# HGRN2 scores in blocks of 32 or 64 tokens, written by column groups of TensorE

## The chip, the cores and the metric

One Trainium2 chip, of which the kernel uses one core. The metric is device time in microseconds (us); three runs of the kernel before have a median of 2869.47 us (2864.01 to 2870.82).

## The reference, cut to what matters

The program is one layer of a diffusion backbone over 256 context and 2048 latent tokens, with four parallel mixers. The change touches the HGRN2 mixer alone, a gated linear recurrence over four heads of 64 channels, in both directions of time:

```
def step(S, inp):
    qc, kc, vc, lf = inp
    b = jnp.cumsum(lf, axis=1)
    ...
    diff = jnp.minimum(b[:, :, None] - b[:, None, :], 0.0)
    decay = jnp.where(lower, jnp.exp(diff), 0.0)
    scores = jnp.einsum('bthk,bshk,btshk->bhts', qc, kc, decay)
    intra = jnp.einsum('bhts,bshv->bthv', scores, vc)
    S = jnp.exp(b_end)[..., None] * S + jnp.einsum('bshk,bshv->bhkv', kc * jnp.exp(b_end[:, None] - b), vc)
    return S, inter + intra
```

A score of query token t and key token s is a sum over channels of q times k times the product of all forget gates between the two tokens.

## The kernel before, in words

The 2304 tokens are five blocks: 256 context tokens and four times 512 latent tokens. The first pass makes q, the forget gates f and the values by matrix products, each in three matmuls (`gemm_cm`, lines 192 to 194: high times high, high times low, low times high part; `gemm_tm`, lines 579 to 581). The HGRN2 stage then calls `hgrn_local` ten times, for five blocks and two pairs of heads. One call holds both heads of a pair side by side, in chunks of 128 tokens: eight chunks of 128 columns for a latent block, four for the context block. The 128 partitions are 64 channels of the forward and 64 of the backward direction.

Within a chunk the scores are built in levels, as in a binary tree. Line 755 makes the level of the diagonal. For level lv from 0 to 6 the tokens are grouped in cells of 2^lv. ScalarE copies the half of q whose query token lies in the other cell of a pair into a zeroed tile z (lines 780 and 781). TensorE multiplies kt by z for each chunk, a full 128 by 128 square in PSUM (line 787). VectorE (forward half) and GpSimd (backward half) multiply kt by the gates, once for each half of the columns (line 791), and VectorE does the same to q (lines 792 and 793). Of each square only the entries whose two tokens lie in sibling cells belong to this level. For levels 0 to 4 VectorE copies them into `at` under a mask (line 808); for levels 5 and 6 ScalarE copies the off-diagonal blocks (line 806). The squares of one level are a tile of 128 by 1024 in PSUM, of which there are two (`psc`).

After level 6, TensorE transposes kt (line 814), multiplies the scores with the values (line 820) and makes the chunk states (line 829).

```
for i in range(hh * m, hh * m + m):
    s_ = slice(i * 128, i * 128 + 128)
    PE.matmul(sc[:, s_], kt[:, s_], z[:, s_], start=True, stop=True)
...
    V.copy_predicated(a3, masks_[:, lv, :].unsqueeze(1).to_broadcast([128, m2, 128]), s3)
```

Two calls are written in step: five steps of one alternate with five of the call before, so that levels 0 to 3 of one stand beside levels 4 to 6 and the tail of the other. The matrix products of the next call's inputs (`prep`) are written behind them. The order in which each engine issues is then set when the program is built, by a scheduler with its own estimate of durations; each engine works through its list in that order. After this stage come the second pass, the S5 mixer, the output product and the MLP, which last to the end.

Of the kernel before, what the change touches and what calls it, by code (L numbers as in the profile page):

```python
# [10 lines left out]
F32 = mybir.dt.float32  # L11
F32R = mybir.dt.float32r
I32 = mybir.dt.int32
AF = mybir.ActivationFunctionType
# [60 lines left out]
def trunk_kernel(ctx, tc, I, O):  # L75
    nc = tc.nc
    V, A, G, PE, SP = nc.vector, nc.scalar, nc.gpsimd, nc.tensor, nc.sync
# [10 lines left out]
    def nm(s):  # L88
        uid[0] += 1
        return f"{s}_{uid[0]}"  # L90
# [13 lines left out]
    def psc():  # L104
        return psums["s"].tile([128, 1024], F32, tag="ps", name=nm("psc"))
# [5 lines left out]
    def const(name, shape, src, dt=F32, pool=None, q=None):  # L111
        t = (pool or cst).tile(shape, dt, tag=name, name=name)
        (q or SP).dma_start(t, src)
        return t
# [620 lines left out]
    def hgrn_local(b, pair, qn, f, vt, p1, qz, Sx, masks_):  # L735
        t0, n, c = BLOCKS[b]
        n2 = 2 * n
        m = n // CH
        m2 = 2 * m
# [5 lines left out]
        kt, q, at = w("kt"), w("q"), w("at")  # L745
# [3 lines left out]
                SP.dma_start(q[64 * d:64 * d + 64, hh * n:(hh + 1) * n], qn[hh * 64:hh * 64 + 64, :n])  # L749
        G.tensor_scalar(kt[:, :n2], f, -1.0, 1.0, ALU.mult, ALU.add)  # L750
        V.tensor_scalar(f, f, F_MIN, None, ALU.max)
        sc = psc()
        for i in range(m2):
            s_ = slice(i * 128, i * 128 + 128)
            PE.matmul(sc[:, s_], kt[:, s_], q[:, s_], start=True, stop=True)
        V.tensor_tensor(q[:, :n2], q[:, :n2], f, ALU.mult)
        A.activation(at[:, :n2], sc[:, :n2], AF.Copy)
        yield
        tcur = f
        tnx = p1.tile([128, 768], F32, tag="tnx", name=nm("tnx"), bufs=2)  # L760
        a3 = at[:, :n2].rearrange("p (m t) -> p m t", t=128)
        for lv in range(7):
            cs = 1 << lv
            mm = n2 // (2 * cs)

            def v4(t, lo_, hi_, half):
                return t[lo_:hi_, :n2].rearrange("p (m two c) -> p m two c", two=2, c=cs)[:, :, half, :]

            tv = tcur.rearrange("p (m two) -> p m two", two=2)

            def tb(lo_, hi_, half):
                return tv[lo_:hi_, :, half:half + 1].to_broadcast([64, mm, cs])

            if lv < len(qz):
                z = qz[lv]
            else:
                z = p1.tile([128, 1024], F32, tag="qzr", name=nm("qzr"), bufs=2)
                G.memset(v4(z, 0, 64, 0), 0.0)
                G.memset(v4(z, 64, 128, 1), 0.0)
            A.activation(v4(z, 0, 64, 1), v4(q, 0, 64, 1), AF.Copy)  # L780
            A.activation(v4(z, 64, 128, 0), v4(q, 64, 128, 0), AF.Copy)
            sc = psc()
            hm = mm // 2
            for hh in range(2):
                for i in range(hh * m, hh * m + m):
                    s_ = slice(i * 128, i * 128 + 128)
                    PE.matmul(sc[:, s_], kt[:, s_], z[:, s_], start=True, stop=True)  # L787
                hs_ = slice(hh * hm, hh * hm + hm)
                for eng, lo_, hi_, half in ((V, 0, 64, 0), (G, 64, 128, 1)):
                    kv = v4(kt, lo_, hi_, half)[:, hs_, :]  # L790
                    eng.tensor_tensor(kv, kv, tb(lo_, hi_, 1 - half)[:, hs_, :], ALU.mult)  # L791
            V.tensor_tensor(v4(q, 0, 64, 1), v4(q, 0, 64, 1), tb(0, 64, 0), ALU.mult)
            V.tensor_tensor(v4(q, 64, 128, 0), v4(q, 64, 128, 0), tb(64, 128, 1), ALU.mult)
            if lv == 6:
                V.tensor_tensor(tot[:, 2 * pair:2 * pair + 2, c0:c0 + m],
                                tv[:, :, 0].rearrange("p (h m) -> p h m", h=2),
                                tv[:, :, 1].rearrange("p (h m) -> p h m", h=2), ALU.mult)
            else:
                nxt = tnx[:, 512 * (lv % 2):512 * (lv % 2) + mm]
                V.tensor_tensor(nxt, tv[:, :, 0], tv[:, :, 1], ALU.mult)  # L800
                tcur = nxt
            s3 = sc[:, :n2].rearrange("p (m t) -> p m t", t=128)
            if lv >= 5:
                for o_ in range(0, 128, cs):
                    x_ = o_ ^ cs
                    A.activation(a3[o_:o_ + cs, :, x_:x_ + cs], s3[o_:o_ + cs, :, x_:x_ + cs], AF.Copy)
            else:
                V.copy_predicated(a3, masks_[:, lv, :].unsqueeze(1).to_broadcast([128, m2, 128]), s3)
            yield
        SP.dma_start(qD[b][:, 2 * pair:2 * pair + 2, :], q[:, :n2].rearrange("p (h t) -> p h t", h=2))  # L810

# [13 lines left out]
        for hh in range(2):  # L825
            h = 2 * pair + hh
            for i in range(m):
                o_ = 512 + (hh * m + i) * 64
# [471 lines left out]
    def pool(stack, name, bufs=1, side="left"):  # L1300
        return stack.enter_context(tc.tile_pool(name=name, bufs=bufs, side=side))
# [20 lines left out]
    with ExitStack() as e1:  # L1322
# [46 lines left out]

        ready = [prep(0), prep(1)]  # L1370
        p1 = pool(e1, "p1")
        masks_ = const("masks", [128, 5, 128], I["masks"], I32, p1, SP)
        qz = [p1.tile([128, 1024], F32, tag=f"qz{lv}", name=f"qz{lv}") for lv in range(3)]
        for z in qz:
            G.memset(z, 0.0)
# [105 lines left out]
    p3 = pool(e5, "p3")  # L1481
    with ExitStack() as e:
        s5_out(1, pool(e, "so1"))
    pad = pool(e5, "pad").tile([128, 16], F32, tag="pad", name="pad")
    G.memset(pad, 0.0)
    h3a = pool(e5, "h3a", 9)
    fs = mlp_up(0, 3, h2, p30, h30, none)
# [129 lines left out]
```

## Time and profile before

| what | us |
|---|---|
| median of three runs | 2869.47 |
| the profiled execution, its own time | 2862.84 |
| its span, first to last instruction | 2860.9 |
| TensorE (PE) busy in the span | 2708.4 |
| VectorE (DVE) busy | 1887.5 |
| ScalarE (ACT) busy | 1108.4 |
| GpSimd (POOL) busy | 920.4 |

The first product of `hgrn_local` starts at 178 us of the span and its last ends at 628 us. In the profile one float32 matmul is two records of MATMUL and two of LDWEIGHTS, so eight chunks are sixteen records. A busy time is the time from a record's start to its modelled end; records overlap, so the pace of TensorE is read from the starts.

### The profile page before, as it was taken

Reading aid. Unit: us, or ns where it says so; the run is one execution under the profiler, and the core shown is the slowest. Engines: PE = TensorE matmul, PEld = TensorE weight load, DVE = VectorE, ACT = ScalarE, POOL = GpSimd, SP = SyncE. Lnnn points to the kernel's source line nnn. Section 1 sums busy time; section 2 is a strip of 40 time slices with the busy share of each in tenths; the row PEclk is TensorE's granted clock in tenths of the full one; section 3 lists DMA queues with packets and bytes.
Section 4 is the critical chain, followed back from the end, with each engine's and each line's share of the span. In section 5 each row is a group of like instructions: output and inputs, shape, how many; then the busy total and the mean of one; then the engine's idle time right before and its main releaser. Section 6 shows DMA issues by size and latency. Waiting matters only on the chain.

```text
span 2860.9 us, 38042 instructions
## 1 busy us (share of the span) xinstructions
PE 2708.4 (95%) x14376; PEld 2257.5 (79%) x14376; DVE 1887.5 (66%) x2766; ACT 1108.4 (39%) x1710; POOL 920.4 (32%) x809
## 2 busy tenths in 40 slices
PE   6798999899999879999999999999999999999998
PEld 3576878887777679987788888788887888888888
DVE  9879678956899976669873475943474334543336
ACT  4645455532333445442422343333343223423323
POOL 4435334612533533343231232211332111411113
PEclk8899999999999979999999999999999999999999
DMA  7784555688886756533333343333343234233333
GB/s 264 282 294 151 188 193 178 229 286 310 299 295 225 241 173 203 174 118 111 111 103 96 125 143 108 111 99 104 114 149 106 99 94 127 90 124 96 96 96 126
DMA packets 186279, 467.17 MB, mean 163 GB/s; under 512 B 40176, under 2 KB 70000, under 8 KB 173040
## 3 DMA queue, kind: packets, MB, share of 16 engines
q1 hardware_dynamic: 183936, 463.56, 48.8%
q8 instruction: 114, 1.87, 0.3%
q10 hardware_dynamic: 2160, 1.18, 0.1%
q14 instruction: 69, 0.57, 0.1%
HBM read 383.47 MB, written 77.53 MB: 161 GB/s over the span
## 4 chain that ended last, share of the span: by engine, by line
PE 62%; DVE 10%; DMA 2%; issue 1%; ACT 0%; SPq 0%; POOL 0%; DVEq 0%; ACTq 0%
PE pg L194 20%; PE pg L193 20%; PE pg L192 20%; DVE x L1184 3%; DVE m L997 1%; DVE whl L162 1%; DMA awt<-in_ada_w_dram 1%; DVE gg L1005 1%; DVE pa L289 0%; PE pb L1051 0%; DVE hh L1014 0%; DVE hh L1013 0%; DVE lo L304 0%; DMA t<-mixD 0%; PE pd L986 0%
## 5 line engine op out<-in xcount | busy, mean ns | idle before, releaser
L192 PE MATMUL pg<-hi,whl 128*128 128x512 f32 (+1 forms) x3488 | 1286.5, 371 | 10.2 <-ACT st L586 4.9
L194 PE MATMUL pg<-hi,whl 128*128 128x512 f32 (+1 forms) x3488 | 1286.2, 370 | 8.4 <-DVE whl L162 8.4
L193 PE MATMUL pg<-lo,whl 128*128 128x512 f32 (+1 forms) x3488 | 1287.0, 370 | 2.3 <-DVE lo L1245 2.3
L160 POOL TENSOR_TENSOR whl<-wraw,whl 128x512 fp32r<-128x512 f32 (+1 forms) x296 | 435.7, 1493 | 1193.5 <-ACT whl L156 1159.9
L192 PEld LDWEIGHTS pg<-hi,whl 128*128 128x128 f32 x3488 | 662.3, 190 | 130.6 <-issue 5.8
L194 PEld LDWEIGHTS pg<-hi,whl 128*128 128x128 f32 x3488 | 662.9, 190 | 125.8 <-DVE whl L162 8.9
L193 PEld LDWEIGHTS pg<-lo,whl 128*128 128x128 f32 x3488 | 663.4, 190 | 120.0 <-issue 6.9
L156 ACT ACTIVATE whl<-wraw 128x1024 fp32r<-128x1024 f32 (+1 forms) x396 | 415.3, 1051 | 588.1 <-PE pg L194 457.0
L162 DVE TENSOR_TENSOR whl<-wraw,whl 128x1024 fp32r<-128x1024 f32 x248 | 310.7, 1254 | 63.1 <-ACT whl L156 61.8
L1257 DVE SCALAR_TENSOR_TENSOR x<-pg,adaT,x 128x512 f32<-128x512 f32 (+1 forms) x168 | 111.8, 669 | 282.9 <-PE pg L194 282.4
L1242 DVE TENSOR_TENSOR t<-t 128x512 f32<-128x512 f32 (+1 forms) x160 | 114.1, 714 | 261.0 <-ACT t L1241 260.3
L1241 ACT ACTIVATE t<-pg 128x512 f32<-128x512 f32 (+1 forms) x160 | 88.7, 554 | 382.3 <-PE pg L194 379.6
L1184 DVE SCALAR_TENSOR_TENSOR x<-x,cvw 128x512 f32<-128x512 f32 (+1 forms) x300 | 216.3, 764 | 0.6
L1245 DVE TENSOR_TENSOR lo<-t,hi 128x512 fp32r<-128x512 f32 (+1 forms) x160 | 142.5, 891 | 35.0 <-ACT hi L1244 34.8
L791 POOL TENSOR_TENSOR kt<-kt,tnx 64x256 f32<-64x256 f32 (+1 forms) x120 | 100.9, 848 | 163.6 <-issue 126.4
L252 POOL TENSOR_TENSOR sq<-sq,sq 128x512 f32<-128x512 f32 (+1 forms) x56 | 87.3, 1559 | 125.6 <-ACT sq L248 125.6
L1244 ACT ACTIVATE hi<-t 128x512 fp32r<-128x512 f32 (+1 forms) x160 | 92.8, 581 | 82.1 <-DVE t L1242 82.1
L1225 DVE SCALAR_TENSOR_TENSOR x<-pg,adaT,x 128x512 f32<-128x512 f32 (+1 forms) x40 | 27.8, 694 | 110.9 <-PE pg L194 110.8
L248 ACT ACTIVATE sq<-x 128x512 f32<-128x512 f32 (+1 forms) x120 | 66.0, 553 | 75.9 <-DVE sq L252 17.4
L787 PE MATMUL psc<-qzr,kt 128*128 128x128 f32 x576 | 74.6, 281 | 10.7 <-DVE kt L791 7.0
L787 PEld LDWEIGHTS psc<-qzr,kt 128*128 128x128 f32 x576 | 70.4, 196 | 14.4 <-POOL kt L791 7.8
L303 ACT ACTIVATE hi<-hm,adaT 128x512 fp32r<-128x512 f32 (+1 forms) x72 | 49.5, 697 | 68.5 <-DVE hm L301 64.5
(373 smaller groups left out, 2919.6 us busy)
## 6 DMA issues: line engine op xcount, KB each, us to landing
wraw<-in_mlp_w_dram SPq DMA_DIRECT2D x328, 512.0 KB, 3.5
whl<-w_p2c_hl SPq DMA_DIRECT2D x32, 1024.0 KB, 7.6
whl<-w_p1c_hl SPq DMA_DIRECT2D x22, 1024.0 KB, 7.7
wraw<-in_w_out_dram SPq DMA_DIRECT2D x40, 512.0 KB, 3.6
awt<-in_ada_w_dram SPq DMA_DIRECT2D x32, 512.0 KB, 5.9
whl<-w_p1t_hl SPq DMA_DIRECT2D x12, 1024.0 KB, 4.9
x<-in_xT_dram SPq DMA_DIRECT2D x16, 512.0 KB, 6.4
aw<-in_ada_w_dram SPq DMA_DIRECT2D x8, 1024.0 KB, 7.2
```

The lines of the kernel that those rows point to most:

```text
L156: A.activation(hi[:, :w], raw[:, :w], AF.Copy)
L160: G.tensor_tensor(lo[:, h_], raw[:, h_], f32(hi[:, h_]), ALU.subtract)
L162: V.tensor_tensor(lo[:, :w], raw[:, :w], f32(hi[:, :w]), ALU.subtract)
L192: PE.matmul(ps[:, :n], wh, xh[:, ts], start=k == 0, stop=False)
L193: PE.matmul(ps[:, :n], wh, xl[:, ts], start=False, stop=False)
L194: PE.matmul(ps[:, :n], wl, xh[:, ts], start=False, stop=k == 7)
L787: PE.matmul(sc[:, s_], kt[:, s_], z[:, s_], start=True, stop=True)
L791: eng.tensor_tensor(kv, kv, tb(lo_, hi_, 1 - half)[:, hs_, :], ALU.mult)
L1184: V.scalar_tensor_tensor(acc[i][:, :n], u2[:, i, k:k + n], cvw[:, i, k:k + 1], acc[i][:, :n], ALU.mult, ALU.add)
L1242: V.tensor_tensor(r, r, r, ALU.mult)
L1245: V.tensor_tensor(lo, r, f32(hi), ALU.subtract)
L1257: V.scalar_tensor_tensor(x8[:, o, ts], ps[:, :n], adaT[:, 40 + o, c:c + 1], x8[:, o, ts], ALU.mult, ALU.add)
```

## The change

The helper `score` replaces the full square of a chunk by 128 / c products of c columns each, where c is 32 for the diagonal and levels 0 to 5, and 64 for level 6. The product of block j takes c tokens of kt as weights (128 partitions by c columns) and c tokens of q or z as moving operand. It writes partitions c*j to c*j + c of PSUM, so the blocks of one chunk lie in different column groups of the array, beneath each other, in c columns of the tile for each chunk. Levels 5 and 6 pair block j with its sibling (j ^ 1). The mask copy then covers 32 columns for each chunk and writes a new tile `al` (128 by 256), and four ScalarE copies behind level 4 bring `al` to the diagonal blocks of `at`. The masks are loaded as four pieces of 32 columns by four DMAs. A padding tile that stands ahead of the MLP's operand tiles grows from 64 to 448 bytes for each partition.

```diff
+        def score(sc, i, z, c, x):
+            for j in range(128 // c):
+                s_, t_ = (slice(i * 128 + c * r, i * 128 + c * r + c) for r in (j, j ^ x))
+                PE.matmul(sc[c * j:c * j + c, c * i:c * i + c], kt[:, s_], z[:, t_], start=True, stop=True)
+        def blocks(sc, c):
+            return sc[:, :c * m2].rearrange("p (m t) -> p m t", t=c)
         sc = psc()
         for i in range(m2):
-            s_ = slice(i * 128, i * 128 + 128)
-            PE.matmul(sc[:, s_], kt[:, s_], q[:, s_], start=True, stop=True)
+            score(sc, i, q, 32, 0)
-        A.activation(at[:, :n2], sc[:, :n2], AF.Copy)
+        A.activation(al[:, :32 * m2], sc[:, :32 * m2], AF.Copy)
...
-                    PE.matmul(sc[:, s_], kt[:, s_], z[:, s_], start=True, stop=True)
+                    score(sc, i, z, max(32, cs), lv >= 5)
...
-                    A.activation(a3[o_:o_ + cs, :, x_:x_ + cs], s3[o_:o_ + cs, :, x_:x_ + cs], AF.Copy)
+                    A.activation(a3[o_:o_ + cs, :, x_:x_ + cs], blocks(sc, cs)[o_:o_ + cs], AF.Copy)
             else:
-                V.copy_predicated(a3, masks_[:, lv, :].unsqueeze(1).to_broadcast([128, m2, 128]), s3)
+                V.copy_predicated(blocks(al, 32), masks_[:, lv, :].unsqueeze(1).to_broadcast([128, m2, 32]),
+                                  blocks(sc, 32))
+            if lv == 4:
+                for o_ in range(0, 128, 32):
+                    A.activation(a3[o_:o_ + 32, :, o_:o_ + 32], blocks(al, 32)[o_:o_ + 32], AF.Copy)
...
-        masks_ = const("masks", [128, 5, 128], I["masks"], I32, p1, SP)
+        masks_ = p1.tile([128, 5, 32], I32, tag="masks", name="masks")
+        for o_ in range(0, 128, 32):
+            SP.dma_start(masks_[o_:o_ + 32], I["masks"][o_:o_ + 32, :, o_:o_ + 32])
...
-    pad = pool(e5, "pad").tile([128, 16], F32, tag="pad", name="pad")
+    pad = pool(e5, "pad").tile([128, 112], F32, tag="pad", name="pad")
```

Because the scheduler's estimates change with the products, the issue order changes too, from the first call of `hgrn_local` to the middle of the context block's MLP. Two places show how. The first is TensorE's list where the second and third call stand side by side and no matrix product of `prep` is between the levels (`psc` is the scores' tile, `qz` and `qzr` are the z tiles, `kt_1902` belongs to the older call). Before:

```order
L755 MATMUL psc_2307<-q_2299,kt_2298 128x128 x8
L787 MATMUL psc_2323<-qzr_2318,kt_1902 128x128 x8
L256 MATMUL pa_2293<-sq_2270,ones 128x512
L787 MATMUL psc_2343<-qz_1538,kt_2298 128x128 x8
L787 MATMUL psc_2365<-qzr_2360,kt_1902 128x128 x8
L787 MATMUL psc_2387<-qz_1539,kt_2298 128x128 x8
L787 MATMUL psc_2409<-qzr_2404,kt_1902 128x128 x8
L787 MATMUL psc_2429<-qz_1540,kt_2298 128x128 x8
L814 MATMUL psc_2447<-ident,kt_1902 128x128 x8
L820 MATMUL psc_2457<-at_1904,vt_837 64x128 x8
L787 MATMUL psc_2483<-qzr_2478,kt_2298 128x128 x8
```

In the changed kernel (its line 758 is the helper's product, 814, 820 and 832 of it are `at<-psc`, `at<-al` and the old line 820):

```order
L758 MATMUL psc_2613<-q_2604,kt_2603 32x32 x32
L758 MATMUL psc_2653<-qzr_2648,kt_2026 32x32 x32
L758 MATMUL psc_2701<-qz_1541,kt_2603 32x32 x32
L758 MATMUL psc_2747<-qzr_2742,kt_2026 32x32 x32
L758 MATMUL psc_2793<-qz_1542,kt_2603 32x32 x32
L758 MATMUL psc_2839<-qzr_2834,kt_2026 64x64 x16
L758 MATMUL psc_2867<-qz_1543,kt_2603 32x32 x26
L256 MATMUL pa_2598<-sq_2575,ones 128x512
L758 MATMUL psc_2867<-qz_1543,kt_2603 32x32 x6
L826 MATMUL psc_2909<-ident,kt_2026 128x128 x8
L832 MATMUL psc_2919<-at_2028,vt_837 64x128 x8
L758 MATMUL psc_2945<-qzr_2940,kt_2603 32x32 x32
```

The levels keep their order and each row of eight squares becomes 32 small products, or 16 at level 6; only the sum of squares (L256) moved, to the inside of a level.

The second place is ScalarE's list at the same point of the program. Before:

```order
L780 ACTIVATE qzr_2404<-q_1903 64x8x64
L781 ACTIVATE qzr_2404<-q_1903 64x8x64
L780 ACTIVATE qz_1538<-q_2299 64x512
L781 ACTIVATE qz_1538<-q_2299 64x512
L287 ACT_TABLE_LOAD
L287 ACTIVATE pa_2293<-pa_2293,epsb 128x512
L780 ACTIVATE qz_1539<-q_2299 64x256x2
L781 ACTIVATE qz_1539<-q_2299 64x256x2
L806 ACTIVATE at_1904<-psc_2365 32x8x32 x4
```

In the changed kernel:

```order
L767 ACTIVATE al_2612<-psc_2613 128x256
L790 ACTIVATE qzr_2834<-q_2027 64x8x64
L791 ACTIVATE qzr_2834<-q_2027 64x8x64
L248 ACTIVATE sq_2586<-x_360_2562 128x512
L790 ACTIVATE qz_1541<-q_2604 64x512
L791 ACTIVATE qz_1541<-q_2604 64x512
L820 ACTIVATE at_2028<-al_2035 32x8x32 x4
L248 ACTIVATE sq_2589<-x_360_2562 128x512
L790 ACTIVATE qz_1542<-q_2604 64x256x2
L791 ACTIVATE qz_1542<-q_2604 64x256x2
L248 ACTIVATE sq_2592<-x_360_2562 128x512
L814 ACTIVATE at_2028<-psc_2747 32x8x32 x4
```

The four new copies of the older call (L820) stand ahead of the z copies of the younger call's level 1 (L790, L791), which were next to those of level 0 before.

## Rows read from the trace of the kernel before

**Rows 1.** The page's first part: busy time, share of the span, records.

```profile
PE 2708.4 (95%) x14376; PEld 2257.5 (79%) x14376; DVE 1887.5 (66%) x2766; ACT 1108.4 (39%) x1710; POOL 920.4 (32%) x809
```

**Rows 2.** Windows: stretch, length; busy PE, PEld, DVE, ACT, POOL; granted clock, DMA.

```profile
178.00:300.00 122.00, 101.00 (x618) 87.08 (x616) 111.85 (x157) 63.52 (x99) 53.08 (x62) 0.94 0.49 176
300.00:360.00 60.00, 58.98 (x347) 51.35 (x348) 38.30 (x64) 29.75 (x51) 20.98 (x24) 1.00 0.67 230
360.00:420.00 60.00, 53.60 (x342) 47.02 (x341) 51.84 (x93) 33.30 (x58) 24.05 (x28) 1.00 0.52 182
420.00:480.00 60.00, 59.47 (x376) 52.66 (x375) 40.54 (x70) 28.04 (x48) 21.25 (x30) 1.00 0.55 186
480.00:628.00 148.00, 131.70 (x1009) 121.08 (x1007) 123.48 (x265) 71.44 (x137) 69.54 (x99) 0.98 0.69 242
```

**Rows 3.** Waits from 178 to 630 us: total us, times, longest.

```profile
POOL kt L791 <- PE psc L787: 77.9, 35, 15.8
...
PE psc L787 <- DVE at L808: 8.0, 7, 3.8
```

**Rows 4.** Groups by line and shape: busy us, mean ns of one, idle before.

```profile
L787 PE MATMUL psc<-qzr,kt 128*128 128x128 f32 x576 | 74.6, 281 | 10.7 <-DVE kt L791 7.0 <-ACT kt L815 2.4 <-DVE at L808 0.9
L787 PE MATMUL psc<-qz,kt 128*128 128x128 f32 x432 | 57.5, 287 | 13.9 <-DVE at L808 7.1 <-DVE kt L791 2.8 <-ACT qz L781 2.1
...
L755 PE MATMUL psc<-q,kt 128*128 128x128 f32 x144 | 18.1, 277 | 3.0 <-POOL kt L750 2.7 <-issue 0.3
```

**Rows 5.** Timeline of TensorE: eight full squares between matrix products (start, us, what).

```profile
196.11 0.39 PE L193 MATMUL pg<-lo,whl 128*128 128x512 f32 x1
196.33 0.39 PE L194 MATMUL pg<-hi,whl 128*128 128x512 f32 x1
196.56 1.95 PE L787 MATMUL psc<-qz,kt 128*128 128x128 f32 x16
198.26 0.48 PE L192 MATMUL pg<-hi,whl 128*128 128x512 f32 x1
```

**Rows 6.** The same view: products in two column groups, between matrix products.

```profile
247.13 0.39 PE L581 MATMUL pg<-whl,hi 128*128 128x512 f32 x1
247.45 1.09 PE L820 MATMUL psc<-at,vt 128*64 128x128 f32 x16
248.48 0.50 PE L580 MATMUL pg<-whl,lo 128*128 128x512 f32 x1
```

**Rows 7.** The same view: products in four column groups of 32, in the S5 mixer.

```profile
693.79 0.40 PE L937 MATMUL pd<-tb,u 128*32 128x128 f32 x8
694.01 0.40 PE L937 MATMUL pd<-tb,dr 128*32 128x128 f32 x8
```

**Rows 8.** Timeline of weight loads: 128 columns each, for products of 32 moving columns.

```profile
659.02 3.76 PEld L893 LDWEIGHTS pd<-u,ta 128*128 128x128 f32 x32
```

**Rows 9.** Groups by shape of the copies out of the scores' tile.

```profile
L808 DVE COPY_PREDICATED at<-masks,psc 128x1024 f32<-128x1024 int32 x40 | 53.3, 1332 | 0.0
L808 DVE COPY_PREDICATED at<-masks,psc 128x512 f32<-128x512 int32 x10 | 7.2, 720 | 0.0
```

**Rows 10.** The same view on ScalarE.

```profile
L806 ACT ACTIVATE at<-psc 32x256 f32<-32x256 f32 x32 | 12.0, 375 | 5.5 <-PE psc L787 5.2
...
L757 ACT ACTIVATE at<-psc 128x1024 f32<-128x1024 f32 x8 | 8.2, 1024 | 6.6 <-PE psc L755 5.1 <-ACT vt L584 1.5
```

**Rows 11.** Windows of line 808 alone: VectorE's busy time in two of the stretches.

```profile
300.00:360.00 60.00, 6.92 (x6) 1.00 0.67 230
...
420.00:480.00 60.00, 8.07 (x6) 1.00 0.55 186
```

**Rows 12.** Windows of line 787 alone in the same two: TensorE, weight loads.

```profile
300.00:360.00 60.00, 13.57 (x112) 13.28 (x112) 1.00 0.67 230
...
420.00:480.00 60.00, 17.76 (x149) 17.50 (x150) 1.00 0.55 186
```

**Rows 13.** The window of the longest run of levels without matrix products.

```profile
272.00:296.00 24.00, 14.74 (x105) 13.88 (x105) 22.63 (x33) 10.37 (x17) 10.58 (x14) 0.86 0.15 44
```

More of the change, by code (lines that the diff above doesn't have):

```diff
@@ L751, in hgrn_local @@
         V.tensor_scalar(f, f, F_MIN, None, ALU.max)
+        al = p1.tile([128, 256], F32, tag="al", name=nm("al"), bufs=2)
+        def score(sc, i, z, c, x):
[4 more added lines that the diff above has]
+            return sc[:, :c * m2].rearrange("p (m t) -> p m t", t=c)
         sc = psc()
         for i in range(m2):
-            s_ = slice(i * 128, i * 128 + 128)
-            PE.matmul(sc[:, s_], kt[:, s_], q[:, s_], start=True, stop=True)
+            score(sc, i, q, 32, 0)
         V.tensor_tensor(q[:, :n2], q[:, :n2], f, ALU.mult)
-        A.activation(at[:, :n2], sc[:, :n2], AF.Copy)
+        A.activation(al[:, :32 * m2], sc[:, :32 * m2], AF.Copy)
         yield
@@ L785, in hgrn_local @@
                 for i in range(hh * m, hh * m + m):
-                    s_ = slice(i * 128, i * 128 + 128)
-                    PE.matmul(sc[:, s_], kt[:, s_], z[:, s_], start=True, stop=True)
+                    score(sc, i, z, max(32, cs), lv >= 5)
                 hs_ = slice(hh * hm, hh * hm + hm)
@@ L801, in hgrn_local @@
                 tcur = nxt
-            s3 = sc[:, :n2].rearrange("p (m t) -> p m t", t=128)
             if lv >= 5:
```

## The prediction

> **What bounds the kernel now.** I read the page's busy times first. TensorE is busy 95% of the span, VectorE 66% [rows 1]; for the whole program TensorE sets the end, so time is won only where its list gets shorter or stops waiting. The change works in the HGRN2 stage, 178 to 628 us, so I then read that stage in windows [rows 2]. The reader is to see two kinds of stretch. From 300 to 360 and 420 to 480 us TensorE is busy 59 of 60 us and VectorE 38 and 41: TensorE leads. In the other 330 us TensorE is busy 286 us and VectorE 287 us: there TensorE waits about 44 us, and VectorE is the busiest engine or its equal (112 of 122 us in the first). Over the stage TensorE is busy 405 of 450 us. The table of waits shows for what the engines wait: GpSimd's kt products wait 77.9 us in total for the scores, and TensorE waits 8.0 us for the mask copies to free a scores' tile [rows 3]. So scores, kt products and mask copies form a loop, and the change shortens two of its three parts.
>
> **Part 1: TensorE.** The scores are 576 + 432 + 144 = 1152 records [rows 4], 72 levels of sixteen (a context level counts as half of one). What a level costs now is read from starts: the matmul ahead of it starts at 196.33, the one behind it at 198.26, 1.93 us, of which 0.23 us is the pace of a 512-column matmul (196.11 to 196.33). So a level costs 1.70 us, 106 ns for each pass of 128 columns [rows 5].
>
> The new products have no row: no product here has 32 weight columns and 32 moving columns. I bound them by the nearest rows. Products in column groups of 32 stand in the S5 mixer: eight records, two passes in four groups, take 0.22 us from start to start [rows 7], 0.11 us for a pass of four groups, the same as one full pass. So the four groups work at once. Those products stream 128 columns, the new ones a quarter. Upper bound: 0.11 us for each pass of four groups, as if fewer columns saved nothing. Lower bound: a quarter, 0.027 us. Between them: weight loads of 128 columns, with products of only 32 columns behind each, follow each other every 3.76 / 32 = 0.118 us [rows 8], 0.011 more than the 0.107 of the load itself. The product is hidden beside the next load and a pass costs its longer side and 0.011. I take that row, as it has the same 32 moving columns: 0.027 + 0.011 = 0.038 us.
>
> The Trainium skill, "TensorE: Matmul & The Clock Gate", Part 1, has a rule against this: starts of matmuls never come closer than about 25 ns, however few columns there are. By it a level's 64 small products would take an estimated 1.6 us and the change would save TensorE nothing. Nothing above rests on that rule; it belongs to the last rival.
>
> To this comes a price for entering and leaving column groups. The products with the values run in two groups: 1.35 us from the matmul ahead to the one behind [rows 6], less 0.23 for that matmul and less 8 passes of 0.107, leaves 0.26 us. I charge it to every level, though some levels stand side by side without it.
>
> A new level of 32-column blocks: 16 passes of 0.038 and 0.26 are 0.87 us, 0.83 saved. Level 6, in blocks of 64 columns: 16 passes of 0.053 + 0.011 and 0.26 are 1.28 us, 0.42 saved. Seven levels of the first and one of the second save 0.78 us on average, 56 us for 72. With the upper bound a level costs 2.02 us, 0.32 more than now, 23 us more for 72.
>
> **Part 2: VectorE.** The mask copy takes 1332 ns for 1024 columns and 720 for 512 [rows 9], 1.195 ns for a column. For 256 columns that line gives 720 - 306 = 414 ns, 31% of now. All 50 copies fall from 60.5 us to some 19.
>
> **Part 3: ScalarE.** It gets four copies for each call from `al` to `at`, of 32 by 256, 375 ns each in the same form [rows 10]: 1.5 us, ten calls 14 us with two of half size. The diagonal's copy shrinks from 1024 ns to about a third. ScalarE is busy 226 of 450 us [rows 2], which hides the total. But the four wait for the last mask copy, and behind them on ScalarE stand the z copies of the younger call (second place of the order): at worst 1.5 us for each call, 15 us. TensorE needs them late, for the product with the values. I take 0 and keep 15 for the range.
>
> **Small parts.** Four mask loads in place of one lie between the same transfers in front of the stage's first level: 0. The wider padding only moves addresses of the MLP's operands: 0, no row prices it. Behind the stage the issue order is different up to the context block's MLP while the work is the same: 0, with 10 us either way.
>
> **The sum, stretch by stretch.** Where TensorE leads, its own saving counts: 112 + 149 records of line 787 [rows 12] are 16.3 levels, with their diagonal levels 18.6; times 0.78 are 14.5 us. Elsewhere I let only VectorE's saving count, since it is the smaller of the two: 60.5 us of mask copies less the 6.92 + 8.07 in those two stretches [rows 11] are 45.5 us, of which 69% go, 31.4 us. TensorE loses there 53.4 levels times 0.78, 41.7 us, so it does not stand in the way. Together 46 us. The profiled execution took 2862.84 us, with 1.9 us around its span, and would take 2817. The median of the runs shown, 2869.47, lies 6.6 us above it; I forecast that median: 2869.5 - 46 = **2823 us**. What is late next in the stage is the elementwise chain, VectorE's q products and GpSimd's kt products.
>
> **The rivals.**
> - *Both savings count everywhere.* TensorE's 56 us fall out, and of its 45 us of waiting about half goes, since the loop around the mask copies is shorter. 78 us, 2791. For it: TensorE's waits in the stage are for that loop. Against it: VectorE would be busier than any engine is now. Chance 0.15.
> - *The chain of kt products holds the other stretches.* A level cannot start before GpSimd has multiplied kt, and those 330 us keep their length. Only the 14.5 us count: 2855. For it: GpSimd's kt products stand first in the waits [rows 3]. Against it: they wait there for the scores themselves, which come earlier. Chance 0.12.
> - *The clock.* In the longest run of levels without matrix products, 272 to 296 us, the granted clock was 0.86 [rows 13], against 0.98 as the mean of the stage's windows [rows 2]. Smaller scores leave the array less to do. If the whole stage fell to 0.86, the 349 us that TensorE keeps would grow by 14%, 48 us, the whole gain: 2871, no change. Against it: the stretches full of matrix products show 1.00. Chance 0.08.
> - *Slower: the pace of issue.* The row of four groups also reads as one weight load and product every 27 ns [rows 7]. If that is the pace at which TensorE can issue them, not the time of its 128 columns, a level keeps 16 times 0.11 us: 23 us more on TensorE, which then leads the whole stage and makes VectorE's saving worthless: 2892. It decides from 0.09 us for a pass, (1.70 - 0.26) / 16, 22.5 ns for each pair. For it: each pass now has four times the instructions. Against it: nothing in the row separates the two readings. It is also how the change would not do what it says: fewer columns, no less time. Chance 0.08.
>
> The 25 ns of the page named above would put this rival, by an estimate of 0.16 us more for each of 72 levels, at 2881. The four-group row's 27 ns agree with it and do not test it; no run here shows smaller products in groups.
>
> **How the numbers follow.** The forecast itself, 2805 to 2845, has 0.57. With the first two rivals that is 0.84 for faster by over 0.3% (8.6 us, about what a measurement of this kernel can tell from no change). The clock has 0.08 and stands for within 0.3%, issue has 0.08 and stands for slower. The range reaches from the first rival, 2790, to 2868, just short of the clock's case: it takes in ScalarE's 15 us and the 10 us of the order, and leaves out the last two rivals and some of the first.
>
> **What would show it.** Right: eight chunks of a 32-column level take 0.7 to 1.1 us from the matmul ahead to the one behind (less 0.23); mask copies of 128 by 256 near 414 ns; the stage's last product ends near 582 us instead of 628; everything behind it has its old length. Wrong: 64 records of a level spread over 1.6 us or more (issue); a granted clock under 0.9 over the stage (clock); TensorE's waits for GpSimd's kt products growing by some 40 us (chain); a different length from the stage's end to the last instruction, by more than 10 us, which none of my parts has.

## The result, and the profile after

The changed kernel takes 2819.64 us (median of four runs, 2818.44 to 2825.11) against 2867.93 us for the kernel before on the same chip: a ratio of 0.9836, 95% interval 0.9818 to 0.9854, 48 us less. The forecast was 2823 us. The total came out within 4 us of it, but not by its own sum: about 25 us come from the HGRN2 stage, where 46 were forecast, and about 24 us from the padding, which was costed at nothing. Two errors of the same size cancelled, so the total is right by luck. What follows shows both.

The page's first part of the changed kernel, against [rows 1]:

```profile
PE 2637.8 (94%) x17544; PEld 2192.0 (78%) x17544; DVE 1844.9 (65%) x2766; ACT 1116.7 (40%) x1750; POOL 912.3 (32%) x809
```

TensorE is busy 71 us less with 3168 more records, VectorE 43 us less, ScalarE 8 us more (the new copies).

The groups by line and shape of the stage (176 to 605 us), against [rows 4, 9, 10]; line 758 is the helper's product, 816 the mask copy, 820 the copy from `al` to `at`:

```profile
L758 PE MATMUL psc<-qz,kt 128*32 128x32 f32 x1728 | 25.3, 211 | 41.1 <-ACT qz L791 15.7 <-DVE al L816 14.4 <-ACT sq L248 4.9
L758 PE MATMUL psc<-qzr,kt 128*32 128x32 f32 x1728 | 24.3, 202 | 4.8 <-POOL kt L800 2.4 <-issue 2.4
...
L816 DVE COPY_PREDICATED al<-masks,psc 128x256 f32<-128x256 int32 x40 | 17.1, 429 | 0.0
...
L820 ACT ACTIVATE at<-al 32x256 f32<-32x256 f32 x32 | 13.2, 414 | 4.0 <-DVE al L816 3.6
...
L816 DVE COPY_PREDICATED al<-masks,psc 128x128 f32<-128x128 int32 x10 | 2.8, 285 | 0.0
```

A mask copy takes 429 ns (414 forecast, 1332 before), all fifty 19.9 us instead of 60.5. The timeline of TensorE gives the price of a level (start, us, what):

```profile
202.10 0.39 PE L194 MATMUL pg<-hi,whl 128*128 128x512 f32 x1
202.33 0.39 PE L192 MATMUL pg<-hi,whl 128*128 128x512 f32 x1
202.65 0.76 PE L758 MATMUL psc<-qz,kt 128*32 128x32 f32 x64
203.34 0.51 PE L193 MATMUL pg<-lo,whl 128*128 128x512 f32 x1
```

From the matmul ahead to the one behind are 1.01 us, less 0.23 for that matmul 0.78 us: 0.87 was forecast, 1.70 it was before [rows 5]. The matmul ahead is followed after 0.32 us instead of 0.23, so entering the column groups costs 0.09; from the first small product to the next large one pass 0.69 us for 64 records, 11 ns for each. The pieces of TensorE's and VectorE's work are as small as forecast. What they are worth is another matter: the stage's last product starts at 604.5 us instead of 627.8, and 582 was forecast. (Here and below the stage's end is the start of that product, 0.3 us ahead of its own end.)

### The profile page after: what moved, and what is told of

The parts are those of the page before. It is cut to its first block, busy times and chain, and to the rows that moved or that the text cites. A ratio compares the mean times of both kernels' runs of the same rounds, so it can differ in the third digit from the quotient of the medians.

```text
span 2818.2 us, 44413 instructions
## 1 busy us (share of the span) xinstructions
PE 2637.8 (94%) x17544; PEld 2192.0 (78%) x17544; DVE 1844.9 (65%) x2766; ACT 1116.7 (40%) x1750; POOL 912.3 (32%) x809
## 4 chain that ended last, share of the span: by engine, by line
PE 58%; DVE 13%; DMA 2%; issue 1%; ACT 1%; POOL 0%; SPq 0%; DVEq 0%; ACTq 0%; POOLq 0%
PE pg L193 19%; PE pg L194 19%; PE pg L192 19%; DVE x L1196 4%; DVE m L1009 1%; DVE whl L162 1%; DMA x<-uD 1%; DVE hh L1026 1%; DVE gg L1017 1%; DVE pa L289 0%; DMA x<-mixD 0%; DVE hh L1025 0%; DVE lo L1257 0%; DMA t<-mixD 0%; DVE pb L289 0%
## 5 line engine op out<-in xcount | busy, mean ns | idle before, releaser
L160 POOL TENSOR_TENSOR whl<-wraw,whl 128x512 fp32r<-128x512 f32 (+1 forms) x296 | 429.7, 1472 | 1185.4 <-ACT whl L156 1145.7
L800 POOL TENSOR_TENSOR kt<-kt,tnx 64x256 f32<-64x256 f32 (+1 forms) x120 | 92.9, 791 | 156.6 <-issue 115.3
L800 DVE TENSOR_TENSOR kt<-kt,tnx 64x256 f32<-64x256 f32 (+1 forms) x120 | 59.5, 519 | 51.9 <-PE psc L758 51.0
L304 DVE SCALAR_TENSOR_TENSOR lo<-hm,adaT,hi 128x512 fp32r<-128x512 f32 (+1 forms) x72 | 67.0, 947 | 5.5 <-ACT hi L303 4.6
```

The costliest lines, as they stand in the source:

```text
L160: G.tensor_tensor(lo[:, h_], raw[:, h_], f32(hi[:, h_]), ALU.subtract)
```

## Experiments on the padding

**The padding alone.** The kernel before with one line of the change; the issue order is the same on every engine.

```diff
-    pad = pool(e5, "pad").tile([128, 16], F32, tag="pad", name="pad")
+    pad = pool(e5, "pad").tile([128, 112], F32, tag="pad", name="pad")
```

> The kernel before with one edit: the padding tile of 448 bytes. All five engines issue in the same order as before. My theory: the 512-column matmuls of the latent MLP whose moving operand lies behind that padding start every 232 ns in the kernel before and every 227 ns in the changed one, and the operand's address alone makes that; some 3840 matmuls by 5 ns are 19 us. So this kernel takes 2848 to 2851 us, 17 to 20 less than before, with its HGRN2 stage ending near 628 us as before. Rival: the gain behind the stage comes from the changed issue order; then this kernel takes what the one before takes, within 4 us, and the pace stays at 232 ns.

Measured: 2843.60 us (six runs) against 2868.01, ratio 0.9922 (0.9907 to 0.9937), 18 to 27 us less: 24 us for a constant. The theory's way is right, the time lies 4 us below its range, and the rival falls. The stage is untouched, its last product comes at 627.0.

**The scores alone.** The changed kernel with the old padding.

```diff
-    pad = pool(e5, "pad").tile([128, 112], F32, tag="pad", name="pad")
+    pad = pool(e5, "pad").tile([128, 16], F32, tag="pad", name="pad")
```

> The changed kernel with the padding of 64 bytes of the kernel before. My theory: the HGRN2 stage ends near 604 us as in the changed kernel, the MLP keeps the pace of 232 ns, and the time is 2842 to 2846 us, 22 to 26 less than before. Rival: the issue order sets what is won behind the stage; then the time stays near 2820 us.

Measured: 2842.72 us (five runs), ratio 0.9914 (0.9901 to 0.9927), the stage's last product at 602.9. This is the theory's range, and the rival falls. The parts add: 24.4 and 25.3 us alone, 48.3 together.

**Which bytes.** The padding moves the buffer `h3a`, the moving operand of the output product and of the MLP's up products. In the program it begins at byte 134656 of each partition plus the padding, and 134656 is a multiple of 256; the weights `whl` begin 192 bytes behind such a multiple, and so does `h3b`, the moving operand of the down products. Three other paddings, and one kernel in which weights and `h3a` move down by 128 bytes together:

```diff
-    pad = pool(e5, "pad").tile([128, 112], F32, tag="pad", name="pad")
+    pad = pool(e5, "pad").tile([128, 32], F32, tag="pad", name="pad")
```

> The changed kernel with a padding of 128 bytes in place of 448: the buffer h3a, the moving operand of the latent MLP's up products, then begins 128 bytes behind a multiple of 256, where the changed kernel has it 192 behind one (as the weights and the other buffer h3b are) and the kernel before 64. Theory A (one of these products takes 227 ns where its moving operand lies at the same place within 256 bytes as its weights, and 232 ns elsewhere): 232 ns each, about 2838 us. Theory B (64 bytes is the one bad place): 227 ns, about 2820 us. Theory C (only the distance of 448 bytes counts, or a place within 1024): 232 ns here and in the runs with 192 and 256 bytes.

```diff
+    pad = pool(e5, "pad").tile([128, 48], F32, tag="pad", name="pad")
```

> The changed kernel with a padding of 192 bytes: h3a begins 64 bytes behind a multiple of 256, as in the kernel before, but 704 behind a multiple of 1024 (before: 576; changed kernel: 960). Theory A (the place within 256 bytes, against the weights') and theory B (64 is the bad place): 232 ns per up product, about 2838 us. Theory C (the place within 1024, 576 alone being bad): 227 ns, about 2820 us.

```diff
+    pad = pool(e5, "pad").tile([128, 64], F32, tag="pad", name="pad")
```

> The changed kernel with a padding of 256 bytes: h3a begins at a multiple of 256. Theory A (same place within 256 bytes as the weights): 232 ns per up product, about 2838 us. Theory B (64 alone is the bad place): 227 ns, about 2820 us.

```diff
-    s5p = cst.tile([128, 3, 16], F32, tag="s5p", name="s5p")
-    A.dma_start(s5p, I["s5_par"])
...
+    shift = cst.tile([128, 16], F32, tag="shift", name="shift")
+    G.memset(shift, 0.0)
...
+        s5p = s5s.tile([128, 3, 16], F32, tag="s5p", name="s5p")
+        A.dma_start(s5p, I["s5_par"])
```

In the last one a tile of 192 bytes leaves the place ahead of the weights and one of 64 takes it. Its issue order differs too (a ninth of TensorE's list), so its pace is read and not its time.

> The changed kernel with everything on the left side, the weights and h3a among it, moved down by 128 bytes: weights and h3a then both begin 64 bytes behind a multiple of 256, while h3b stays at 192. Theory A (equal places of weights and moving operand are fast): the up products (moving operand h3a) stay at 227 ns and the down products (h3b) go to 232 ns. Theory B (the moving operand's own place counts, whatever the weights'): the up products go to 232 ns and the down products stay at 227 ns. In either case some 18 us more than the changed kernel, about 2838 us; neither speaks of the total alone.

The view is windows of TensorE alone (stretch, length, busy us and records, granted clock, DMA share, GB/s): the first row lies inside a run of up products, 36 us long, the second inside a run of down products, 32 us long. The count takes in records of 0.39 us that reach over an end of the window, so the pace is (36 + 0.39) us / 156 = 233 ns and not 36 / 156. Before:

```profile
2765.00:2801.00 36.00, 36.00 (x156) 1.00 0.28 88
2725.00:2757.00 32.00, 32.00 (x143) 1.00 0.30 99
```

The changed kernel:

```profile
2724.00:2760.00 36.00, 36.00 (x160) 1.00 0.27 90
2683.00:2715.00 32.00, 32.00 (x143) 1.00 0.28 99
```

The kernel before with the padding of the changed one:

```profile
2750.00:2786.00 36.00, 36.00 (x161) 1.00 0.31 97
```

The changed kernel with a padding of 128 bytes:

```profile
2750.00:2786.00 36.00, 36.00 (x156) 1.00 0.26 88
```

Padding of 192 bytes:

```profile
2727.00:2763.00 36.00, 36.00 (x160) 1.00 0.28 88
```

Padding of 256 bytes:

```profile
2732.00:2768.00 36.00, 36.00 (x159) 1.00 0.26 88
```

Weights and `h3a` moved together:

```profile
2738.00:2774.00 36.00, 36.00 (x160) 1.00 0.27 88
2697.00:2729.00 32.00, 32.00 (x138) 1.00 0.31 99
```

TensorE is never idle and the clock is full in all of them; the same matmuls come at another pace. The mean from start to start, over some 3000 up products of each kernel (pauses of over 260 ns left out), against where the moving operand lies within 256 bytes, seen from the weights:

| kernel | up products: place, ns | down products: place, ns | time, us |
|---|---|---|---|
| before (padding 64) | -128, 232.9 | 0, 227 | 2867.9 |
| before, padding 448 | 0, 226.9 | 0, 227 | 2843.6 |
| padding 128 | -64, 233.3 | 0, 227 | 2851.6 |
| padding 192 | 0, 226.9 | 0, 227 | 2825.6 |
| padding 256 | +64, 229.0 | 0, 227 | 2828.6 |
| changed kernel (padding 448) | 0, 226.9 | 0, 227 | 2819.6 |
| weights and h3a moved | 0, 226.9 | +128, 233 | 2832.7 |

The last row decides between theories A and B: `h3a` lies where it was slow before (64 behind a multiple of 256), the weights lie there too, and the up products are fast, while `h3b`, which did not move, has become slow. So the distance of the two operands counts, not a place of its own (the tiles that moved together with the weights are not told apart from them; the weights are the one other operand that these matmuls read), and it repeats with 256 bytes (padding 192 and 448 agree, 704 and 960 behind a multiple of 1024: theory C falls). Theory A had only two values; the +64 row is a miss, it costs 2 ns and not 5. There are 3840 matmuls with `h3a` (24 for each of 8 output and 32 up units, four blocks): 3840 times 6.0 ns are 23 us of the 24 measured.

The kernel with 128 bytes is 9 us slower than the one with the old 64 at the same pace, and the one with 192 is 6 us slower than the one with 448. The traces put both into the HGRN2 stage, which stands ahead of every tile that the padding moves: its last product comes at 602.9 us with 64 bytes and at 612.1 with 128, at 604.5 with 448 and at 609.3 with 192 (603.0 with 256), in one and the same issue order. So this stage varies by 9 us from one execution to the next, and a stage's end that is read from one trace is no surer than that. Why it varies is not shown.

## Experiments on the stage

**Two that moved the order.** TensorE's and VectorE's savings were first taken back one at a time. Four products of a constant ahead of each level's scores give TensorE back about what a level saves:

```diff
+        def fill(sc):
+            for j in range(m2 // 2):
+                PE.matmul(sc[:, 512 + 128 * j:640 + 128 * j], ident, ones, start=True, stop=True)
...
+            fill(sc)
```

> The changed kernel with four products of constants (128 by 128 by 128, identity by ones, into the unused half of the scores' tile, read by nobody) ahead of each level's scores, two in the context block: about 0.85 us of TensorE for a level, 61 us over the stage, which gives back all that the small scores save there. In the changed kernel the granted clock was at its lower level for 92 us between 176 and 605 us, in the kernel before for 20 us of its stage. My theory: that is where half of the gain of 46 us went that the forecast gave the stage; with the constants the lower level falls back under 40 us and the stage ends at 595 to 610 us although TensorE does 61 us more. Rival: the elementwise chain on VectorE and GpSimd holds the stage and the clock costs nothing; then the constants fill waits only in part, the stage ends 10 to 30 us later (615 to 635 us), and a clock that comes back shows no gain.

Measured: 2870.70 us, ratio 1.0002 (0.9991 to 1.0014), stage end 623.5, in the rival's range. And the mask copies three times, 1.29 us instead of 0.43:

```diff
-                V.copy_predicated(blocks(al, 32), masks_[:, lv, :].unsqueeze(1).to_broadcast([128, m2, 32]),
-                                  blocks(sc, 32))
+                for _ in range(3):
+                    V.copy_predicated(blocks(al, 32), masks_[:, lv, :].unsqueeze(1).to_broadcast([128, m2, 32]),
+                                      blocks(sc, 32))
```

> The changed kernel with each mask copy of levels 0 to 4 made three times, about 1.29 us in place of 0.43, what the copy of the full squares took. VectorE's saving of some 42 us is given back, TensorE's stays. My theory, by the forecast's sum, in which VectorE's saving carries two thirds of the stage's gain: 15 to 30 us slower than the changed kernel, 2835 to 2850 us. Rival: TensorE's saving makes the gain by itself; then it takes 2820 to 2828 us.

Measured: 2867.39 us, ratio 1.0001 (0.9989 to 1.0013), outside both ranges, stage end 645.8, 18 us later than before. Either half taken back seems to take everything. But the scheduler set another order for both kernels, inside the stage and behind it (the residual additions of the first output block, line 1225 of the kernel before, end at 1028.9 and 1033.0 us there, at 998.9 before), so neither run measures a size, and a theory built on them (A below) did not last.

**Three that keep the order.** So the order of the kernel before was kept, and operands were changed in the finished instruction list: each score product replaced by four (or two) small ones, or the mask copies narrowed, or both. Waits and signals stay with the first and the last of the four; ScalarE's copies keep their sizes and read the scores where they now lie.

```diff
+            if pe and i.opcode == "Matmult" and line in (755, 787):
...
+                for j in range(128 // c):
...
+                        ins=[_ap(z, c * (j ^ x), (1, c)), _ap(kt, c * j, (1, c))], outs=[o],
...
+            if line == 808 and i.opcode == "CopyPredicated":
+                if dve:
+                    ins = [_ap(m, 0, (0, n), (1, 32)), _ap(s, 0, (1, 32 * n))]
+                    out = _ap(out, 0, (1, 32 * n))
+                elif pe:
+                    ins[1] = _ap(s, 0, (0, 4), (1, 32 * n))
```

(`_ap` gives an operand another offset and another list of steps and counts; `pe` and `dve` are the two cuts.)

> The kernel before, with its issue order and its padding kept on every engine; only the operands are changed once the order stands: each score product becomes the changed kernel's small products, the mask copies keep their 1024 columns (they read the 256 written ones four times). The output is not the reference's. It is the part of TensorE alone, without the reordering that spoils the two runs with fillers and with threefold mask copies. The prediction's sum would give 14.5 us (stretches where TensorE led): 2853 us, the stage's last product near 613. Theory A (TensorE and VectorE bind in turns inside each level, so that one part alone is worth little): 0 to 8 us less, stage end 620 to 628. Theory B (the granted clock gives the gain back): over 60 us at half clock in the stage (before 20) and no gain or a loss.

> The kernel before, order and padding kept; only the mask copies are narrowed from 1024 to 256 columns once the order stands, the scores stay products of 128 by 128. The output is not the reference's. It is the part of VectorE alone. The prediction's sum would give 31.4 us: 2837 us, stage end near 596. Theory A (both bind in turns): 4 to 15 us less, stage end 613 to 624. Theory B (clock): the scores are the old ones, so the clock stays as before, and the whole 31 us show.

> Both cuts in the issue order of the kernel before: small score products and mask copies of 256 columns. The output is not the reference's; the four copies from al to at are left out. Against the run of the scores alone with the old padding (2842.7 us, stage end 602.9, in the changed issue order). Theory A (the missing half went to waits inside the levels, whatever the order): 20 to 28 us less than before, stage end 600 to 608, about 2844 us, clearly more than the two parts alone add up to. Theory O (the new issue order and the four copies cost the missing half): 40 us or more less than before, stage end 580 to 590, below 2830 us. Theory B (clock): as theory A in time, with over 80 us at half clock in the stage.

| | time, us | against before | stage's last product |
|---|---|---|---|
| before | 2867.64 | | 627.8 |
| small scores alone | 2856.28 | 0.9951 (0.9933 to 0.9969) | 621.1 |
| narrow masks alone | 2851.39 | 0.9941 (0.9922 to 0.9961) | 612.9 |
| both | 2841.36 | 0.9899 (0.9879 to 0.9919) | 602.1 |
| changed kernel, old padding | 2842.72 | 0.9914 (0.9901 to 0.9927) | 602.9 |

By the intervals small scores alone bring 9 to 19 us, narrow masks alone 11 to 22, both 23 to 35, and the changed kernel with the old padding 21 to 28. So each part is worth something alone, and within these intervals they add; the ends of the stage (6.7, 14.9 and 25.7 us earlier, each from one trace, with the 9 us above on them) agree. Theory A was right on the size for both cuts together and on the stage's ends to within 0.1 us of its ranges, but its point, that both are "clearly more than the two parts alone add up to", falls. Both cuts in the old order give what the changed kernel gives in its own: theory O falls. Only the sum of order and copies is shown, near 0; one could pay for the other.

Where the gains lie is read from windows that end where a new call of `hgrn_local` begins on GpSimd (columns as in [rows 2]). The four stretches from the third call to the seventh, before:

```profile
258.60:299.90 41.30, 27.51 (x182) 23.78 (x180) 38.58 (x62) 21.09 (x34) 18.18 (x23) 0.88 0.11 33
299.90:357.40 57.50, 56.38 (x336) 49.21 (x337) 35.87 (x61) 27.70 (x47) 19.29 (x23) 1.00 0.65 227
357.40:398.70 41.30, 36.34 (x244) 32.01 (x242) 38.53 (x67) 23.87 (x41) 19.35 (x23) 1.00 0.44 143
398.70:456.80 58.10, 56.66 (x336) 49.30 (x337) 35.91 (x64) 27.38 (x49) 18.07 (x23) 1.00 0.56 195
```

Small scores alone:

```profile
258.50:298.60 40.10, 20.41 (x534) 16.70 (x533) 37.91 (x59) 20.02 (x33) 18.16 (x24) 0.61 0.11 35
298.60:351.10 52.50, 50.41 (x688) 41.44 (x689) 36.53 (x60) 27.44 (x47) 18.41 (x24) 0.97 0.69 244
351.10:394.20 43.10, 32.66 (x595) 25.90 (x594) 39.98 (x68) 23.81 (x41) 18.31 (x23) 0.80 0.44 145
394.20:447.50 53.30, 50.30 (x688) 41.32 (x689) 36.42 (x63) 27.22 (x49) 16.77 (x24) 0.97 0.61 214
```

Narrow masks alone:

```profile
256.40:293.70 37.30, 26.55 (x171) 23.36 (x170) 33.37 (x61) 20.49 (x34) 17.47 (x24) 0.82 0.12 37
293.70:352.80 59.10, 58.05 (x336) 50.87 (x337) 31.74 (x60) 28.13 (x48) 18.20 (x23) 0.97 0.63 222
352.80:392.20 39.40, 36.01 (x244) 31.95 (x242) 35.47 (x66) 23.18 (x41) 18.13 (x23) 1.00 0.45 148
392.20:450.40 58.20, 56.65 (x336) 49.29 (x337) 32.50 (x65) 27.34 (x49) 18.00 (x23) 1.00 0.55 195
```

Both:

```profile
255.00:293.00 38.00, 21.64 (x534) 17.40 (x532) 35.13 (x62) 20.51 (x34) 18.73 (x23) 0.59 0.12 37
293.00:344.80 51.80, 50.45 (x688) 41.50 (x689) 31.44 (x58) 27.49 (x47) 19.78 (x24) 0.95 0.70 249
344.80:385.50 40.70, 31.28 (x595) 24.70 (x593) 35.72 (x68) 23.86 (x41) 17.50 (x23) 0.87 0.47 151
385.50:439.10 53.60, 50.21 (x688) 41.23 (x689) 32.21 (x63) 27.10 (x49) 18.94 (x24) 0.97 0.61 212
```

The two kinds of stretch are there as the prediction had them (differences of 1 or 2 us between single traces say little). In the second and fourth, where TensorE leads, small scores take 5.0 and 4.8 us and narrow masks nothing (+1.6 and +0.1). In the first and third narrow masks take 4.0 and 1.9 us, and small scores 1.2 and -1.8. In the third, both together leave 40.7 of 41.3 us, although TensorE is busy 31.3 there, VectorE 35.7 and the others less: no engine is full, which leaves the chain from one to the next.

These four are not the whole stage. From the seventh call to the last product, before, with small scores, with narrow masks and with both:

```profile
456.80:627.80 171.00, 154.17 (x1155) 141.40 (x1154) 143.96 (x302) 83.69 (x158) 79.18 (x110) 0.98 0.69 241
447.50:621.10 173.60, 140.71 (x2324) 122.11 (x2322) 143.96 (x303) 83.61 (x158) 82.08 (x110) 0.89 0.69 239
450.40:612.90 162.50, 152.58 (x1156) 141.12 (x1154) 130.26 (x300) 83.45 (x158) 75.01 (x110) 0.98 0.72 254
439.10:602.10 163.00, 138.74 (x2323) 120.12 (x2322) 129.59 (x302) 83.33 (x158) 78.17 (x110) 0.91 0.71 254
```

Here narrow masks take 8.5 us, more than half of all they bring, and small scores nothing (+2.6), though TensorE is busy 13.5 us less.

The table of waits over the stage points to that chain. Narrow masks alone (total us, times, longest):

```profile
POOL kt L791 <- PE psc L787: 80.4, 33, 15.9
DVE kt L791 <- PE psc L787: 51.3, 20, 9.8
```

Small scores alone:

```profile
PEld psc L787 <- issue: 48.2, 43, 7.2
...
PE psc L787 <- DVE at L808: 18.5, 9, 4.1
PE psc L787 <- DVE kt L791: 17.3, 7, 7.1
```

And before, the same three of them that grew:

```profile
DVE kt L791 <- PE psc L787: 41.7, 17, 9.8
...
PE psc L787 <- DVE kt L791: 9.8, 6, 2.8
PE psc L787 <- DVE at L808: 8.0, 7, 3.8
```

VectorE, with less to copy, waits 9.6 us longer for the scores, and GpSimd keeps its wait of some 80 us for them [rows 3]. TensorE, with less to multiply, waits 18 us longer for VectorE's mask copies and kt products. So each engine hands a part of what it saves to the other as a wait. The largest row that grew with small scores, 48.2 us of idle weight loads with no cause that the profile shows (8.8 before), stays open, and no run changed GpSimd's products, so the third part of the loop is argued from its waits alone.

**The clock.** The half clock (1.2 GHz of 2.4) grew with the small scores: its intervals in the stage sum to 21 us before, 113 with the small scores alone, 96 with both and 92 in the changed kernel; the first of the four stretches, where TensorE has the least to do, has 31, 31 and 27 of these last three. The last run asks what that costs. The order is kept; four products of a constant are put behind a level's scores where no 512-column matmul follows.

```diff
+    for i, k in zip(mms, mms[1:]):
+        if i.debug.lineno == 758 and k.outs[0].memref != i.outs[0].memref and k.debug.lineno not in gemm:
+            ends.add(i.name)
```

> The changed kernel with its issue order kept on every engine; once the order stands, four products of a constant with itself (128 by 128, about 0.85 us at full clock) are put behind the last score product of a level at the 52 places where no matrix product of 512 columns follows on TensorE, that is where TensorE is about to wait. They wait for nothing and nobody waits for them but TensorE's next instruction; they fill a part of the score tile that nobody reads. 44 us of products into some 100 us of waits and half clock. It asks what the half clock (92 us in the stage, about 22 us of longer products by the accounting of starts) costs. Theory A (it lies beside VectorE, which is busy in those stretches): time within 6 us of the changed kernel, 2814 to 2826, though the half clock falls below 60 us. Theory B (it costs its 22 us): 2800 to 2812 us, faster than both kernels. Theory C (the fillers themselves get in the way of the next level): 2830 us or more.

Measured: 2833.22 us (2825.45 to 2840.86), ratio 0.9891 (0.9871 to 0.9911), against 0.9836 for the changed kernel. The half clock in the stage fell from 92 to 27 us and the stage's last product came at 614.2 instead of 604.5. The stretch that was slowest, in the changed kernel:

```profile
255.00:290.00 35.00, 13.74 (x394) 11.11 (x394) 34.37 (x54) 21.30 (x36) 21.18 (x25) 0.61 0.13 40
```

With the fillers:

```profile
255.00:290.00 35.00, 21.07 (x520) 18.35 (x519) 34.37 (x54) 20.15 (x34) 21.44 (x26) 0.85 0.13 40
```

Theory B falls: the clock came back and no time with it; the time is in theory C's range. In this stretch VectorE is busy 34.4 of 35 us either way, so TensorE's clock costs nothing there. Elsewhere the fillers' own price lies over what the clock gave back; the two are not told apart, so what half clock costs in the other stretches stays open.

No version beat the changed kernel; the one with 192 bytes of padding (0.9849, 0.9821 to 0.9878) can't be told from it.

## Why the prediction was right, and where its steps were wrong

**Small products in column groups: right.** 0.78 us against 0.87. The forecast chose the row with 32 moving columns over the upper bound of 0.11 us for each pass. The rival of issue pace needed 0.09 us for a pass; the 16 passes of a level take 0.69 us, 0.043 each, its way out of the groups included. By the 25 ns between starts of the Trainium skill, "TensorE: Matmul & The Clock Gate", Part 1, a level's 64 records would take an estimated 1.6 us; the trace has 0.69. The rule does not hold across four column groups, and the same page's Part 3 says that products in different tiles of the array overlap.

**Mask copies: right.** 429 ns against 414 for 256 columns, fifty of them 19.9 us against some 19.

**ScalarE and the order: right at 0 as a sum.** The run with both cuts has neither the four copies nor the new order and takes 2841.36 us, the changed kernel with the old padding 2842.72. In the changed kernel TensorE waits 15.7 us for the z copies (the first row of L758 above; 2.1 in [rows 4]), which the order may have won back elsewhere; the two are not told apart.

**The sum, stretch by stretch: wrong, 46 us for 25.** The step that failed is "Elsewhere I let only VectorE's saving count, since it is the smaller of the two", 31.4 us. Narrow masks alone brought 14.9 us at the stage's end, 11 to 22 by the interval of their time. A saving that is the smaller of two is not therefore won whole: it is won only while its engine is the last to be ready, and in those 330 us, as far as the waits show, the levels pass from TensorE to VectorE and GpSimd and back, none of them full. The signs were there. The stretch 178 to 300 was counted as VectorE's (112 of 122 us) though it joins a part where TensorE was busy 73 of 81 us and one where it was busy 28 of 41; windows cut at the start of each call show the two apart. And [rows 3] had VectorE's partner GpSimd waiting 77.9 us for scores: the prediction used that row against its rival of the kt chain. The rival's sign did not come: TensorE's products wait 6.3 us for GpSimd's kt products in the changed kernel and its weight loads 13.0 (10.3 before), not 40 us more. Yet its 2855 us lie 12 us from the 2842.7 of the scores alone, and the forecast's 2823 lie 20 from it. The smaller term, 14.5 us where TensorE leads, came to 9.8 in the two windows above (the time of small scores alone, 9 to 19 us less, allows either): TensorE's busy time fell by 6.0 and 6.4 us there, and its idle time grew by 1.0 and 1.6.

**The padding: wrong, 0 for 24 us.** "The wider padding only moves addresses of the MLP's operands: 0, no row prices it." No row of the trace before priced a move, but its windows did hold two paces for one kind of matmul, 233 ns for the up products and 227 for the down ones (156 records in 36 us, 143 in 32). That difference could have been read, and it puts a price on a move of the slower operand: 3840 times 6 ns, 23 us. The prediction bounded its new products from both sides; it did not do so for the one part that had no price at all.

**The rivals.** Both savings everywhere (2791): no. The clock: its mechanism and its sign came, a granted clock of 0.61 in the longest run of levels and of 0.89 over the stage (the sign was under 0.9), but not its price of 48 us; in that run of levels VectorE was busy throughout, and what the rest cost is open. The pace of issue: no, as above. The length behind the stage, which was to stay, is 20 us shorter, by more than the 10 us that the prediction named as a sign of being wrong, which "none of my parts has": it is the padding.

## What to carry to other kernels

Cut windows where the program changes what it does, and let a saving count only where its engine is full; where no engine is full, measure the chain from one engine to the next, since an engine that gets faster there may mostly wait longer. When one kind of matmul shows two paces in a trace, compare the addresses of its operands before anything else: here a few hundred bytes of padding were worth as much as the rewritten products. To take a scheduled kernel apart, change operands with the order kept; runs in which the scheduler is free to reorder mix two effects. Before a stage's end is compared between two traces, see how far it lies apart in traces of the same order.

## What the runs showed of the hardware

- A matmul of 512 columns takes 226.9 ns from start to start where its moving operand and its weights lie at the same place within 256 bytes of a partition, 229.0 with the operand 64 bytes further, 233 at 128 bytes or 64 the other way, with the clock at 1.00 and TensorE never idle. Other distances were not tried, and why it is so is not shown.
- Sixty-four records of 32 by 32 in four column groups take 0.69 us, 11 ns for each; entering the groups behind a large matmul costs 0.09 us.
- With small products in place of full squares the granted clock fell from 0.88 to 0.61 in the first of the four stretches, where few large ones are near, and from 1.00 to 0.97 in the second and fourth, which are full of them.
